# Gate matrix of a PEER layer: one-hots and gates from fp32 to bf16, three exact gate parts, written in pairs of columns

## The chip, the cores and the metric

One core of a Trainium2 chip runs the whole program. The time is device microseconds from launch to the end of one execution. Before the change it is 3040.93 us, the median of 3 runs (3038.23 to 3045.83). The engines are named as in the profile: PE is the matrix engine (PEld its weight loads), DVE the vector engine, ACT the scalar engine, POOL the general-purpose engine, and SP the engine that issues most DMAs.

## The reference, cut to what matters

The program is two transformer blocks in fp32 over 512 tokens of width 1024. Only the last part, the PEER layer of the second block, is touched. For every token, 8 retrieval heads choose 16 experts each out of 16384 = 128 x 128, so a token has 128 slots; slot s names an expert by two indices (i, j) between 0 and 127 and carries a softmax weight, its gate.

```python
gates = jax.nn.softmax(best_s, axis=-1)
...
act = jax.nn.gelu(jnp.einsum('td,thkd->thk', xb, u).astype(jnp.float32))
w = (gb * act).astype(xb.dtype)
return jnp.einsum('thk,thkd->td', w, v)
```

The kernel computes this for 384 of the 512 tokens (three blocks of 128, `NDENSE = 3`) in dense form: it multiplies the tokens with the first matrix of all 16384 experts, applies gelu, multiplies with a gate matrix that is zero where a token has not chosen an expert, and multiplies with the second matrix of all experts. For one token the gate matrix is 128 x 128: entry (i, j) is the sum over the 128 slots of onehot(i)[s] * gate[s] * onehot(j)[s], which is one matmul over the slots. The last 128 tokens fetch their chosen rows by indirect DMA ("gathers") instead.

## The kernel before

The program is written as straight code, and the order on each engine comes from a scheduler that simulates the timeline; blocks marked high priority go first when they are ready, and `issue_after` keeps an instruction behind a named one. The code runs through these stages at the end:

- *Retrieval* (`retrieve`, L1238, and `decode`): scores, the two top-16 searches and the expert indices, on DVE for the most part, with the dense products of experts 0 to 14 beside it on PE.
- *Gate stage*. `slots_T` (L1360) transposes the slots of one token block (i, j, gate) on PE, so that slots lie on partitions and tokens on columns, and ACT copies the result to SBUF as `slT`, in fp32. `gate_matrix` (L1370) then goes through 12 blocks of 32 tokens, each in 8 groups of 4 tokens (96 groups in all, "quads" below). For a quad it needs, per token, a 128 x 128 one-hot matrix of j (`ohB`) and one of i times the gate (`ohA`). Even quads take form A: DVE makes both one-hots in one instruction (L1382, 1024 columns), and ACT multiplies the one of i by the gate, one token at a time (L1384). Odd quads take form D: DVE makes the one-hot of j (L1386, 512 columns) and then, per token, the one of i times the gate in one instruction (L1388). PE multiplies the two, 4 matmuls per quad in fp32 (L1391; the trace has two records for each), into a PSUM tile `pg` of one bank, of which there are 2. ACT copies it to a staging tile (L1393). After 8 quads SP writes the 2 MB staging tile to DRAM (`gd`).
- Beside the gate stage PE makes the dense products of experts 19 to 39 (`expert_act`, L1397: 24 matmuls of 384 columns each, fp32r, L271 to L273, from weights that ACT and POOL split into a high and a low part, L245 and L248). `peer` (L1430) spaces them: gates have high priority, and the product of expert j is kept behind a gate quad that lies 10 quads back (`NLAG`). The last three products come after the last quad.
- *Expert stage*. `open_v` frees the buffers of the gate stage; then for each of 128 groups of experts the gates are read back (`gread`, L1466), multiplied with the activations (L1414), and multiplied with the second matrix. The gathers run beside it. The first `gread` needs all 12 writes to `gd`.

The lines that set the pace of the gate stage:

```python
if GATED[q] == "A":
    nc.vector.tensor_tensor(one, iota(2), sl[:, 0:2, k:k + 4, None]...., op=ALU.is_equal)
    for r in range(4):
        nc.scalar.activation(A4[:, r], one[:, 0, r], AF.Copy, scale=sl[:, 2, ...])
else:
    nc.vector.tensor_tensor(one[:, 1:2], iota(1), sl[:, 1:2, k:k + 4, None]...., op=ALU.is_equal)
    for r in range(4):
        nc.vector.tensor_scalar(A4[:, r], self.iota, ..., op0=ALU.is_equal, op1=ALU.mult)
for r in range(4):
    last = nc.tensor.matmul(p[:, r, :], A4[:, r], one[:, 1, r], start=True, stop=True)
```

Of the kernel before, what the change touches and what calls it, by code (L numbers as in the profile page):

```python
# [11 lines left out]
BF16 = mybir.dt.bfloat16  # L12
U32 = mybir.dt.uint32
AF = mybir.ActivationFunctionType
# [33 lines left out]
GATED = "ADADADAD"  # L48
# [121 lines left out]
class Prog:  # L170
# [1189 lines left out]
    def slots_T(self, i):  # L1360

        nc = self.nc
# [3 lines left out]
        t_ = self.B([128, 3, 128], f"slT{i}", 1)  # L1366
        nc.scalar.activation(t_, p, AF.Copy)
        return t_

    def gate_matrix(self, slT, gd):  # L1370

        nc = self.nc
        for b in range(NDENSE * 4):
            st = self.b("gstage", [128, 128, 32])
            for q in range(8):
                p = self.b("pg", [128, 4, 128])
                t_ = b * 32 + q * 4
                sl, k = slT[t_ // 128], t_ % 128
                A4, one = self.b("ohA", [128, 4, 128]), self.b("ohB", [128, 2, 4, 128])
                iota = lambda n: self.iota[:, None, None, :].to_broadcast([128, n, 4, 128])  # L1380
                if GATED[q] == "A":
                    nc.vector.tensor_tensor(one, iota(2), sl[:, 0:2, k:k + 4, None].to_broadcast([128, 2, 4, 128]), op=ALU.is_equal)  # L1382
                    for r in range(4):
                        nc.scalar.activation(A4[:, r], one[:, 0, r], AF.Copy, scale=sl[:, 2, k + r:k + r + 1])  # L1384
                else:
                    nc.vector.tensor_tensor(one[:, 1:2], iota(1), sl[:, 1:2, k:k + 4, None].to_broadcast([128, 1, 4, 128]), op=ALU.is_equal)  # L1386
                    for r in range(4):
                        nc.vector.tensor_scalar(A4[:, r], self.iota, sl[:, 0, k + r:k + r + 1], sl[:, 2, k + r:k + r + 1],  # L1388
                                                op0=ALU.is_equal, op1=ALU.mult)
                for r in range(4):  # L1390
                    last = nc.tensor.matmul(p[:, r, :], A4[:, r], one[:, 1, r], start=True, stop=True)  # L1391
# [145 lines left out]
def body(tc, I, out, dbg=None, manual=False):  # L1537
    nc = tc.nc
    with ExitStack() as es:
# [121 lines left out]
        P.open(eq1, "retrieve", "xs 7 gb keys q; sc 5; mux 1; ts 2; ti 2; bs 2; bc 2; wk 3; cand 1; tif 1; ab 1; bit 2; cm 1; cu 2; cuf 1; ef 1; gate 1; sel0 1; sel1 1")  # L1661
# [5 lines left out]
        def open_q2():  # L1667
            eq1.close()
            P.open(eg, "gate", "gstage 2; ohA 4; ohB 3")
# [22 lines left out]
```

## Time and profile before

| what | value |
|---|---|
| median of 3 runs | 3040.93 us |
| profiled execution, its own time | 3040.9 us |
| its span (first to last instruction) | 3039.1 us |
| mean granted PE clock | 0.989 of full speed |
| PE / DVE / ACT / POOL busy over the span | 97% / 61% / 41% / 44% |

The profile is of one execution. A busy share is an average over stages that have different limits, so the rows below are cut to the gate stage, which lies between 1935 and 2122 us. "Idle before" is the time in which an engine stood still directly before an instruction, and the arrow names what it waited for. Matmuls overlap, so the time that one occupies PE is the distance between two starts, not its duration; the same holds for DVE instructions that follow each other without a wait.

### The profile page before, as it was taken

The page shows a single profiled execution, that of the slowest core. Times are in us where ns is not written, and L with a number is a line of the kernel's source. Part 1 is how long each engine was busy: PE and PEld are TensorE (multiplying, and loading weights), DVE is VectorE, ACT ScalarE, POOL GpSimd, SP SyncE. Part 2 cuts the span into 40 slices and gives each one's busy share as a digit, 9 for nine tenths or more (in the row PEclk, how much of TensorE's full clock was granted, in tenths as well). Part 3 has the DMA queues.
Part 4 walks back from the last instruction along what each step waited for, and adds up shares of the span by engine and source line. Part 5 has one row for each costly group of instructions (what it writes and reads, how often), then busy time and mean ns, then how long its engine had stood idle before and what let it go on. Part 6 is the DMA issues. An engine that isn't in the chain of part 4 may idle for free.

```text
span 3039.1 us, 40262 instructions
## 1 busy us (share of the span) xinstructions
PE 2938.0 (97%) x15129; PEld 2540.3 (84%) x15129; DVE 1867.7 (61%) x3017; ACT 1245.4 (41%) x2120; POOL 1352.4 (44%) x926
## 2 busy tenths in 40 slices
PE   7998998999999999999999999989999999999998
PEld 6877787888878887888888888888899999999887
DVE  4237664444133663355532489898678877777898
ACT  5455654222232453244432344576333333333333
POOL 3223213222234662233332344422677777777765
PEclk9998999999999999999999999999999999999999
DMA  4220003333332212322233432355988888898987
GB/s 155 63 63 15 1 30 103 97 97 97 97 107 88 63 46 73 108 83 81 82 105 114 130 97 88 125 190 195 303 299 296 311 312 302 289 324 300 320 321 264
DMA packets 174355, 473.60 MB, mean 156 GB/s; under 512 B 15057, under 2 KB 64593, under 8 KB 172625
## 3 DMA queue, kind: packets, MB, share of 16 engines
q1 hardware_dynamic: 137296, 336.80, 34.0%
q0 software_dynamic: 36864, 134.23, 12.5%
q8 instruction: 119, 1.95, 0.3%
q14 instruction: 76, 0.61, 0.1%
HBM read 439.49 MB, written 31.46 MB: 155 GB/s over the span
## 4 chain that ended last, share of the span: by engine, by line
PE 78%; issue 6%; DVE 5%; DMA 5%; ACT 3%; POOL 3%; SPq 0%; POOLq 0%; DVEq 0%; ACTq 0%
PE acc L271 15%; PE acc L272 15%; PE acc L273 15%; DMA urow<-ev,ei 3%; PE A L273 3%; PE A L272 3%; PE A L271 3%; PE B L272 3%; PE B L271 3%; PE B L273 3%; PE pg L1391 2%; PE i L810 2%; POOL urow L1339 1%; DMA rawx<-ev 1%; PE lev L987 1%
## 5 line engine op out<-in xcount | busy, mean ns | idle before, releaser
L248 POOL TENSOR_TENSOR lo<-raw,hi 128x1024 fp32r<-128x1024 f32 x224 | 558.1, 2493 | 946.3 <-ACT hi L245 920.5
L271 PE MATMUL acc<-u,hi 128*128 128x512 f32 (+3 forms) x2344 | 857.6, 367 | 4.0 <-DVE sil L912 1.5
L272 PE MATMUL acc<-u,hi 128*128 128x512 f32 (+3 forms) x2344 | 856.8, 366 | 0.2 <-DVE u L477 0.2
L273 PE MATMUL acc<-u,lo 128*128 128x512 f32 (+3 forms) x2344 | 856.9, 366 | 0.0
L245 ACT ACTIVATE hi<-raw 128x1024 fp32r<-128x1024 f32 x447 | 472.3, 1057 | 901.2 <-PE acc L272 457.4
L248 DVE TENSOR_TENSOR lo<-raw,hi 128x1024 fp32r<-128x1024 f32 x223 | 316.1, 1417 | 297.3 <-ACT hi L245 297.0
L271 PEld LDWEIGHTS acc<-u,hi 128*128 128x128 f32 (+1 forms) x2344 | 443.8, 190 | 59.0 <-issue 2.7
L272 PEld LDWEIGHTS acc<-u,hi 128*128 128x128 f32 (+1 forms) x2344 | 444.1, 189 | 54.7 <-issue 2.7
L273 PEld LDWEIGHTS acc<-u,lo 128*128 128x128 f32 (+1 forms) x2344 | 444.0, 189 | 48.7 <-issue 0.6
L1347 DVE SCALAR_TENSOR_TENSOR urow<-urow,h4row 128x1024 f32<-128x1024 f32 x128 | 200.8, 1575 | 94.5 <-DMA urow<-eu,ei 94.3
L1357 DVE SCALAR_TENSOR_TENSOR po<-urow,act,po 128x1024 f32<-128x1024 f32 x127 | 188.9, 1487 | 66.3 <-DMA urow<-ev,ei 65.4
L1339 POOL DMA_INDIRECT urow<-eu,ei x128 | 188.4, 1472 | 32.9 <-issue 21.4
L1417 ACT ACTIVATE wh<-wf 128x384 fp32r<-128x384 f32 x128 | 67.2, 526 | 312.4 <-PE D L272 246.4
L1339 POOL DMA_INDIRECT urow<-ev,ei x128 | 171.2, 1337 | 43.8 <-DVE po L1357 18.0
L248 POOL TENSOR_TENSOR lox<-rawx,hix 128x1024 fp32r<-128x1024 f32 x53 | 134.8, 2543 | 92.7 <-ACT hix L245 92.5
L1391 PE MATMUL pg<-ohB,ohA 128*128 128x128 f32 x768 | 105.1, 286 | 19.0 <-ACT gstage L1393 17.1
L1391 PEld LDWEIGHTS pg<-ohB,ohA 128*128 128x128 f32 x768 | 98.7, 197 | 24.4 <-ACT gstage L1393 20.9
L1418 DVE TENSOR_TENSOR wl<-wf,wh 128x384 fp32r<-128x384 f32 x128 | 98.8, 773 | 6.8 <-ACT wh L1417 5.1
L1384 ACT ACTIVATE ohA<-ohB,slT 128x128 f32<-128x128 f32 x192 | 61.4, 392 | 41.8 <-DVE ohB L1382 41.7
L1414 DVE TENSOR_TENSOR wf<-eact,gread 128x384 f32<-128x384 f32 x98 | 67.0, 684 | 17.0 <-DMA gread<-gd 15.9
L1388 DVE TENSOR_SCALAR ohA<-iota,slT 128x128 f32<-128x128 f32 x192 | 76.6, 461 | 0.0
L245 ACT ACTIVATE hix<-rawx 128x1024 fp32r<-128x1024 f32 x53 | 55.7, 1052 | 27.4 <-DMA rawx<-ev 27.4
(574 smaller groups left out, 5511.1 us busy)
## 6 DMA issues: line engine op xcount, KB each, us to landing
raw<-ut SPq DMA_DIRECT2D x128, 512.0 KB
raw<-ev SPq DMA_DIRECT2D x75, 512.0 KB
rawx<-ev SPq DMA_DIRECT2D x53, 512.0 KB
raw<-w_ret SPq DMA_DIRECT2D x48, 512.0 KB
gd<-gstage SPq DMA_DIRECT2D x12, 2048.0 KB
gread<-gd SPq DMA_DIRECT2D x32, 768.0 KB
raw<-w_gu SPq DMA_DIRECT2D x44, 512.0 KB
raw<-w_hg SPq DMA_DIRECT2D x32, 512.0 KB
```

Source lines behind the costliest of these rows:

```text
L245: self.nc.scalar.activation(hi, raw, AF.Copy)
L248: r = eng.tensor_tensor(lo, raw, hi.bitcast(F32), op=ALU.subtract)
L271: mm(out, a[0], b[0], start=start, stop=False)
L272: mm(out, a[0], b[1], start=False, stop=False)
L273: return mm(out, a[1], b[0], start=False, stop=stop).ins
L1339: r = nc.gpsimd.indirect_dma_start(out=u, out_offset=None, in_=src, in_offset=bass.IndirectOffsetOnAxis(ap=ei[:, s:s + 1], axis=0))
L1347: nc.vector.scalar_tensor_tensor(u, u, 1.0, row, op0=ALU.mult, op1=ALU.mult, accum_out=act[:, s:s + 1])
L1357: nc.vector.scalar_tensor_tensor(o, u, act[:, s:s + 1], o, op0=ALU.mult, op1=ALU.add)
L1388: nc.vector.tensor_scalar(A4[:, r], self.iota, sl[:, 0, k + r:k + r + 1], sl[:, 2, k + r:k + r + 1], op0=ALU.is_equal, op1=ALU.mult)
L1391: last = nc.tensor.matmul(p[:, r, :], A4[:, r], one[:, 1, r], start=True, stop=True)
L1417: nc.scalar.activation(wh, wf, AF.Copy)
L1418: nc.vector.tensor_tensor(wl, wf, wh.bitcast(F32), op=ALU.subtract)
```

## The change

Two quads (8 tokens) now share their one-hots. `slots_T` leaves the indices as bf16 (`ijT`, exact, being below 256) and splits the gate into three bf16 parts whose sum is the fp32 gate (`gT`): ACT rounds the rest to bf16, DVE subtracts, twice. Once for 128 tokens ACT writes indices and gate parts again with every value twice side by side (`ij`, `g3`), so that the innermost run of every DVE operand is two neighbouring bf16 elements. For 8 tokens DVE then makes both one-hots in one instruction (2048 columns of bf16) and multiplies the one of j by each of the three gate parts (three instructions of 1024 columns). PE runs, per token, three bf16 matmuls with the same one-hot of i as weights, and adds them up in PSUM. The finished quads go to the tile `pg` or `psc` in turn, which makes 4 banks. ACT no longer multiplies by the gate; form A and form D are gone.

```diff
-        t_ = self.B([128, 3, 128], f"slT{i}", 1)
-        nc.scalar.activation(t_, p, AF.Copy)
-        return t_
+        ij, g3 = self.B([128, 2, 128], f"ijT{i}", 1, BF16), self.B([128, 3, 128], f"gT{i}", 1, BF16)
+        nc.scalar.activation(ij, p[:, 0:2], AF.Copy)
+        r = self.b("grest", [128, 128])
+        nc.scalar.activation(r, p[:, 2], AF.Copy)
+        for w in range(3):
+            nc.scalar.activation(g3[:, w], r, AF.Copy)
+            if w < 2:
+                r_ = r
+                r = self.b("grest", [128, 128])
+                nc.vector.tensor_tensor(r, r_, g3[:, w], op=ALU.subtract)
+        return ij, g3
...
+        io = self.b("iotab", [128, 128], BF16)
+        nc.vector.tensor_copy(io, self.iota)
+        pairs = lambda a: a.rearrange("p n (c e) -> p n c e", e=2)
...
+            if b % 4 == 0:
+                ij, g3 = self.b("ij", [128, 16, 2, 8, 2], BF16), self.b("g3", [128, 3, 128, 2], BF16)
+                ij_, g3_ = slT[b // 4]
+                for w in range(2):
+                    nc.scalar.activation(ij[:, :, w], ij_[:, w].rearrange("p (n r) -> p n r", r=8)[:, :, :, None].to_broadcast([128, 16, 8, 2]), AF.Copy)
+                nc.scalar.activation(g3, g3_[:, :, :, None].to_broadcast([128, 3, 128, 2]), AF.Copy)
             for q in range(8):
...
+                k = b % 4 * 32 + q * 4
+                if q % 2 == 0:
+                    one, gb = self.b("ohA", [128, 16, 128], BF16), self.b("ohB", [128, 3, 8, 128], BF16)
+                    nc.vector.tensor_tensor(pairs(one), pairs(io[:, None, :].to_broadcast([128, 16, 128])),
+                                            ij[:, k // 8].rearrange("p w r e -> p (w r) e")[:, :, None, :].to_broadcast([128, 16, 64, 2]),
+                                            op=ALU.is_equal)
+                    for w in range(3):
+                        nc.vector.tensor_tensor(pairs(gb[:, w]), pairs(one[:, 8:16]),
+                                                g3[:, w, k:k + 8, None, :].to_broadcast([128, 8, 64, 2]), op=ALU.mult)
+                p = self.b("pg" if q % 2 else "psc", [128, 4, 128])
                 for r in range(4):
-                    last = nc.tensor.matmul(p[:, r, :], A4[:, r], one[:, 1, r], start=True, stop=True)
+                    for w in range(3):
+                        last = nc.tensor.matmul(p[:, r, :], one[:, q % 2 * 4 + r], gb[:, w, q % 2 * 4 + r],
+                                                start=w == 0, stop=w == 2)
...
-            P.open(eg, "gate", "gstage 2; ohA 4; ohB 3")
+            P.open(eg, "gate", "gstage 2; iotab 1; ij 1; g3 1; ohA 2; ohB 2")
```

The rest of a split, `grest`, lies in a buffer of the retrieval pool, whose memory the gate pool takes over.

## Rows read from the trace of the kernel before

**Rows 1.** Page, busy us and share of the span and instructions of each engine.
```profile
PE 2938.0 (97%) x15129; PEld 2540.3 (84%) x15129; DVE 1867.7 (61%) x3017; ACT 1245.4 (41%) x2120; POOL 1352.4 (44%) x926
```
**Rows 2.** Windows: length, busy PE, PEld, DVE, ACT, POOL (instructions), PE clock, DMA, GB/s.
```profile
1970.00:1990.00 20.00, 17.38 (x127) 16.84 (x126) 19.02 (x34) 14.07 (x35) 4.80 (x3) 1.00 0.60 224
2090.00:2110.00 20.00, 16.32 (x112) 15.58 (x110) 18.12 (x31) 13.74 (x35) 5.30 (x2) 0.92 0.45 158
2200.00:2300.00 100.00, 100.00 (x508) 91.12 (x507) 76.72 (x95) 35.38 (x49) 74.62 (x42) 1.00 0.86 303
```
**Rows 3.** Groups by line, 1935 to 2122 us: busy, mean ns | idle before.
```profile
L1391 PE MATMUL pg<-ohB,ohA 128*128 128x128 f32 x768 | 105.1, 286 | 19.0 <-ACT gstage L1393 17.1 <-ACT ohA L1384 1.3
L1388 DVE TENSOR_SCALAR ohA<-iota,slT 128x128 f32<-128x128 f32 x192 | 76.6, 461 | 0.0
L1382 DVE TENSOR_TENSOR ohB<-iota,slT 128x1024 f32<-128x1024 f32 x48 | 60.0, 1251 | 8.1 <-PE pg L1391 6.5 <-ACT slT L1367 1.1
L1393 ACT ACTIVATE gstage<-pg 128x512 f32<-128x512 f32 x96 | 53.6, 585 | 8.6 <-PE pg L1391 8.2
L272 PE MATMUL acc<-u,hi 128*128 128x384 f32 x130 | 45.0, 346 | 0.0
L1386 DVE TENSOR_TENSOR ohB<-iota,slT 128x512 f32<-128x512 f32 x48 | 43.8, 912 | 6.1 <-ACT ohA L1384 3.6 <-PE pg L1391 1.2 <-issue 1.2
L248 POOL TENSOR_TENSOR lo<-raw,hi 128x1024 fp32r<-128x1024 f32 x17 | 43.2, 2541 | 129.7 <-ACT hi L245 129.7
```
**Rows 4.** Timeline of DVE, two quads without a wait: start, us, engine, line, operation.
```profile
1979.21 1.21 DVE L1382 TENSOR_TENSOR ohB<-iota,slT 128x1024 f32<-128x1024 f32 x1
1980.35 1.10 DVE L1388 TENSOR_SCALAR ohA<-iota,slT 128x128 f32<-128x128 f32 x4
1981.37 0.68 DVE L1386 TENSOR_TENSOR ohB<-iota,slT 128x512 f32<-128x512 f32 x1
1981.97 1.21 DVE L1382 TENSOR_TENSOR ohB<-iota,slT 128x1024 f32<-128x1024 f32 x1
```
**Rows 5.** Timeline, the same DVE line beside a POOL instruction.
```profile
1976.18 2.42 POOL L248 TENSOR_TENSOR lo<-raw,hi 128x1024 fp32r<-128x1024 f32 x1 [6.14 <-ACT hi L245]
...
1975.43 3.26 DVE L1388 TENSOR_SCALAR ohA<-iota,slT 128x128 f32<-128x128 f32 x4
```
**Rows 6.** Timeline of DVE, first and last work of the gate stage, next work behind.
```profile
1935.14 2.75 DVE L1382 TENSOR_TENSOR ohB<-iota,slT 128x1024 f32<-128x1024 f32 x1 [1.15 <-ACT slT L1367]
2117.51 1.12 DVE L1388 TENSOR_SCALAR ohA<-iota,slT 128x128 f32<-128x128 f32 x4
2134.51 1.03 DVE L1414 TENSOR_TENSOR wf<-eact,gread 128x384 f32<-128x384 f32 x2 [15.88 <-DMA gread<-gd]
```
**Rows 7.** Timeline of PE, products of an expert, a run of gate matmuls.
```profile
2094.77 0.34 PE L271 MATMUL acc<-u,hi 128*128 128x384 f32 x1
2094.94 0.34 PE L272 MATMUL acc<-u,hi 128*128 128x384 f32 x1
...
2099.17 1.95 PE L1391 MATMUL pg<-ohB,ohA 128*128 128x128 f32 x16
```
**Rows 8.** Timeline of DVE in the retrieval, three instructions of 128 columns.
```profile
1916.97 0.27 DVE L1288 TENSOR_TENSOR gate<-bs 128x128 f32<-128x128 f32 x1
1917.16 0.22 DVE L1297 TENSOR_SCALAR cm<-bc 128x128 uint32<-128x128 uint32 x1
1917.30 0.23 DVE L1298 TENSOR_SCALAR cu<-bc 128x128 uint32<-128x128 uint32 x1
```
**Rows 9.** Groups by line and shape, whole span, weight loads: busy, mean ns | idle.
```profile
L620 PEld LDWEIGHTS <-identb 128*128 128x128 bf16 x32 | 3.2, 99 | 2.6 <-issue 1.7
L1365 PEld LDWEIGHTS pslT<-ident,sel 128*128 128x128 f32 x6 | 0.8, 154 | 5.4 <-ACT sel L1323 3.5 <-ACT slT L1367 1.7
```
**Rows 10.** Timeline of ACT, first copy of transposed slots, first products with the gate.
```profile
1934.63 0.47 ACT L1367 ACTIVATE slT<-pslT 128x384 f32<-128x384 f32 x1
1941.12 1.27 ACT L1384 ACTIVATE ohA<-ohB,slT 128x128 f32<-128x128 f32 x4
```

More of the change, by code (lines that the diff above doesn't have):

```diff
@@ L47 @@
 IN_ORDER = ((0, 0), (0, 1), (0, 2), (0, 3), (1, 0), (1, 1), (1, 2), (1, 3))
-GATED = "ADADADAD"
 NBESIDE = 15
@@ L1370, in gate_matrix @@
+        return ij, g3
     def gate_matrix(self, slT, gd):
         nc = self.nc
+        io = self.b("iotab", [128, 128], BF16)
+        nc.vector.tensor_copy(io, self.iota)
+        pairs = lambda a: a.rearrange("p n (c e) -> p n c e", e=2)
         for b in range(NDENSE * 4):
             st = self.b("gstage", [128, 128, 32])
-            for q in range(8):
[L1376 to L1389, printed above, removed]
@@ L1660, in body @@
         eq1 = ExitStack()
-        P.open(eq1, "retrieve", "xs 7 gb keys q; sc 5; mux 1; ts 2; ti 2; bs 2; bc 2; wk 3; cand 1; tif 1; ab 1; bit 2; cm 1; cu 2; cuf 1; ef 1; gate 1; sel0 1; sel1 1")
+        P.open(eq1, "retrieve", "xs 7 gb keys q; sc 5; mux 1; ts 2; ti 2; bs 2; bc 2; wk 3 grest; cand 1; tif 1; ab 1; bit 2; cm 1; cu 2; cuf 1; ef 1; gate 1; sel0 1; sel1 1")
         P.banks("A psc; C pslT; B pg")
```

## The prediction

> **What bounds the kernel now.** I read the page's busy shares first: PE is at 97% over the span [rows 1], so a change that frees PE looks welcome. The windows cut that down. In the expert stage, 2200 to 2300, PE is busy for all of 100 us; in the gate stage PE is at 17.38 of 20 us, and the engine near its limit is DVE, 19.02 of 20, with ACT at 14.07 [rows 2]. So the stage that the change touches is set by another engine than the page names.
>
> The groups of that stage confirm it. DVE has 48 instructions of 1024 columns, 48 of 512 and 192 of 128, busy for 60.0, 43.8 and 76.6 us, and stands still for only 8.1 + 6.1 = 14.2 us [rows 3]. From its first gate instruction to the end of its last, 1935.14 to 2118.63, are 183.5 us [rows 6].
>
> I split these 183.5 us by distances between starts. Two quads in a row cost 1.14 us (1979.21 to 1980.35), 1.02 and 0.60, together 2.76 [rows 4]; 48 times that is 132.5. Idle is 14.2. What is left, 36.8 us, is something that only some instructions pay. One group of four, 1.10 us long when alone [rows 4], takes 3.26 where a POOL split of 2.42 us runs beside it [rows 5], which is 2.16 more. There are 17 such splits in the stage [rows 3], and 17 x 2.16 = 36.7. So DVE is made of work 132.5, blocking by POOL 36.8 and idle 14.2, and the first two are no one's slack.
>
> What the end of this stage costs the program is one for one. The next DVE work, at 2134.51, waits for a read of the gates [rows 6], which needs the last quad written to DRAM, and behind it PE has no gap into which a delay could go [rows 2]. I add any shift of the stage's end to the whole time.
>
> **The change part by part.** *DVE, two quads.* One compare of 2048 bf16 columns, three products of 1024. No row shows a two-operand bf16 instruction, so I bound it. From 0.60 us for 512 fp32 columns and 1.14 for 1024 [rows 4] a column costs 1.055 ns. If a bf16 column costs the same, the four take 1.14 + 1024 x 0.001055 = 2.22, and 3 x 1.14, together 5.64 us for two quads. If bytes decide, they are the instructions of 1024 and 512 fp32 columns: 1.14 + 3 x 0.60 = 2.94. The trace has a hint that DVE can do two results in a step: the one-operand instruction of 128 columns follows the one before after 0.14 us, the two-operand one of 128 columns needs 0.19 [rows 8], where the fp32 slope for 64 columns is 0.07. I take 2.94, since the operands are laid out in pairs of neighbours that fill one 4-byte word, and keep 5.64 as a rival. A third value below 2.94 would need four results in a step; no row excludes it, and it enters the faster rival. So 48 x 2.94 = 141.1 us, which is 8.6 more than the 132.5 of now. The count of instructions falls from six to four for two quads, but the columns make up for it.
>
> The Trainium skill, "VectorE: DVE Perf Modes", section "Mode 2×_1P — pack two bf16 into one 32-bit read", says that a two-operand instruction gets two results in a cycle if all operands are 16-bit with step one, and one result otherwise. No run so far shows it; by it the pairs would give the 2.94, and a layout without pairs the 5.64.
>
> *Blocking by POOL.* The 17 splits stay. All DVE instructions of a pair now have two operands in SBUF; the two-operand form is blocked like the other now (the means of L1382 and L1386, 1251 and 912 ns, lie above their 1.21 and 0.68 alone [rows 3, 4]). I leave 36.8 us. Below, the blocking could shrink if a packed read leaves room; above, it could hit no more than 17 times 2.42.
>
> *Extra DVE work.* Six subtractions for the three parts and one copy of the table, 7 x 0.19 [rows 8] = 1.4 us.
>
> *PE.* Now 768 records. A run of 16 takes 1.95 us, less the duration of the last, 0.28, over 15 distances: 0.11 us each [rows 7, 3], 85 us in all. The products beside them come every 0.17 us [rows 7], some 387 of them (three groups of about 130 [rows 3]), 66 us. After it there are 96 x 12 = 1152 bf16 matmuls of 128 columns. By columns alone 0.17 / 3 = 0.057 us each; at most the 0.11 of the fp32 records, since each still loads its own weights. An isolated bf16 load is 99 ns and an fp32 one 154 [rows 9]; 0.11 scaled by that is 0.07, which I take: 81 us, and with 66 beside it 147 us in 183. PE is then nearer to 80% than 90% of the stage, and that gain goes nowhere as long as DVE is later: its cover is DVE's 2.94 + 36.8 / 48 = 3.71 us for two quads against PE's 24 x 0.07 + 66 / 48 = 3.06.
>
> The Trainium skill, "TensorE: Matmul & The Clock Gate", section "LDWEIGHTS (loading the stationary operand)", prices a load by its columns, 128 / 1.2 GHz = 107 ns, whatever the contraction; by that 1152 loads would be 123 us where its section on fast weight load would halve them. Rows 9 show a shorter bf16 load, but none back to back.
>
> *ACT and banks.* ACT loses 192 products of the gate and gets five small copies and three widening ones for each 128 tokens; it has 6 of 20 us free now [rows 2], so nothing is counted. With it go the waits of DVE on ACT's `ohA`, 3.6 us, and on PE's `pg`, 6.5 + 1.2 [rows 3]; the second bank takes the 17.1 us that PE waits for the copies out of PSUM [rows 3]. But the new buffers hold two pairs, and DVE must wait for PE's 24 matmuls of the pair before the last, in an order that mixes them with the products of 0.17. And the widened indices and gates have one buffer, so twice, at each new 128 tokens, DVE waits for ACT's refill. I take 5 us of idle, between 0 and the 14.2 of now.
>
> *Start.* Now ACT's first copy of transposed slots begins at 1934.63 and DVE starts 0.5 us later; the first products with the gate on ACT come at 1941.12 [rows 10, 6]. After it a chain of rounding and subtracting between ACT and DVE, three rounds long, stands ahead of the first product with a gate part, and the rest of a split lies in memory that the new one-hot buffers may take over, which then wait for the third block's chain. At ACT's 0.5 us and DVE's 0.27 [rows 10, 8] a round is under 1 us. I take 2 us, between 0 and 5.
>
> *Sum.* 141.1 + 36.8 + 1.4 + 5 + 2 = 186.3 us against 183.5: 2.8 later. The profiled execution took 3040.9 us, of which 1.8 lie outside its span of 3039.1, the median of the runs being 3040.93. So 3040.9 + 2.8 = 3044 us. With idle and start at their ends (0 and 0, 14.2 and 5) the stage is 179.3 to 198.5 us, the time 3037 to 3056.
>
> **The rivals.** *Columns, not bytes.* If DVE doesn't pack, the stage is 48 x 5.64 = 270.7, + 36.8 + 1.4 + 2, nothing idle: 311 us, 127 more, 3168 us. For it speaks that no packed two-operand instruction is in the trace; against it the layout in pairs and rows 8. Slower.
>
> *Weight loads bind PE.* At 0.11 us a matmul PE needs 127 + 66 = 193 us, and starts some 6 us after DVE: 199, or 15 more, 3056 us. It decides from 0.10 us a matmul on, where PE's two quads cost DVE's 3.71. For it speaks that every matmul loads weights anew, three times the same; against it the shorter load of rows 9.
>
> *DVE falls below PE.* If the packed instructions cost less than their bytes, or POOL blocks them for less, DVE's 178 us shrink until PE's 147 bind, with 6 us of start and a tail of quads without products beside them (the window at 2090 to 2110 is of that kind, clock 0.92 [rows 2]): some 160 us, 23 less, 3018 us. For it speaks that nothing in the trace shows these forms; against it that fp32 instructions of both kinds paid the full price of a POOL split.
>
> **How the numbers follow.** The measurement of this kernel can tell about 0.3%, 9.1 us, from no change: faster is below 3031.8, slower above 3050. The forecast (DVE stays the bound, 3037 to 3056) has 0.50, the unpacked rival 0.12, the weight loads 0.16, the faster one 0.22. Of the forecast 0.41 lies within the bound, 0.02 below and 0.07 above; of the weight loads 0.04 within; of the faster one 0.02. So faster 0.22, same 0.47, slower 0.31. The range goes from 3015, a little under the faster rival's value, to 3064, which holds the weight loads with a few us of start; left out are the unpacked case and a little at the ends. The likeliest one's own range is 3037 to 3056.
>
> **What would show it.** Starts of DVE's new instructions 1.14 and 0.60 us apart: bytes decide; 2.2 and 1.14: columns. DVE still some 2.2 us longer beside each POOL split. Distances of bf16 matmuls near 0.07 us, and PE idle in the stage grown to 30 us or more with DVE as what it waits for. First to last gate instruction of DVE about 186 us, and behind it the same distances to the first read of the gates as now. I am wrong if DVE has more than 20 us of idle in the stage, if the gate matmuls come 0.1 us apart, or if the expert stage changes its length by more than the shift.

## The result: 0.7% slower, and the profile after

The changed kernel takes 3062.56 us (median of 4 runs, 3061.87 to 3067.23), the kernel before beside it 3043.38 (4 runs, 3038.23 to 3046.05). The ratio is 1.0068, 95% interval 1.005 to 1.0087. The forecast was 3044: no change that can be told, where the kernel became slower. The time lies inside the range of 3015 to 3064, and above the likeliest case's own range of 3037 to 3056.

The profiled execution took 3067.23 us, with a span of 3065.4, which is 26.3 more than before. It is the longest of the four; between the medians lie 19.2 us. The page's busy shares (answer to [rows 1]) hardly tell the two apart:

```profile
PE 2934.2 (96%) x15513; PEld 2525.9 (82%) x15513; DVE 1879.1 (61%) x2928; ACT 1197.3 (39%) x1949; POOL 1358.1 (44%) x926
```

The windows do (answer to [rows 2], columns as there; the third is later by about the shift):

```profile
1970.00:1990.00 20.00, 15.04 (x149) 13.74 (x148) 17.38 (x18) 7.06 (x12) 4.82 (x2) 0.93 0.47 167
2090.00:2110.00 20.00, 18.85 (x170) 16.72 (x170) 17.46 (x22) 7.59 (x14) 3.27 (x2) 0.84 0.33 132
2225.00:2325.00 100.00, 100.00 (x507) 91.04 (x506) 75.44 (x94) 35.27 (x48) 74.14 (x42) 1.00 0.87 302
```

DVE fell from 19.02 and 18.12 busy us to 17.38 and 17.46, and PE's granted clock from 1.00 and 0.92 to 0.93 and 0.84. Over the eight windows of 20 us from 1950 to 2110 the clock's mean is 0.885, where it was 0.99. It has two levels, 1.2 and 2.4 GHz; 0.885 is a mixture in time. The expert stage is as full as before. The groups of the gate stage, 1935 to 2146 (answer to [rows 3], columns as there), name who waits for whom:

```profile
L1402 DVE TENSOR_TENSOR ohB<-ohA,g 128x1024 bf16<-128x1024 bf16 x144 | 110.4, 822 | 1.6
...
L1398 DVE TENSOR_TENSOR ohA<-iotab,ij 128x2048 bf16<-128x2048 bf16 x48 | 70.2, 1464 | 18.1 <-PE pg L1407 14.8 <-PE psc L1407 2.1 <-ACT ij L1392 0.8
L1407 PE MATMUL psc<-ohB,ohA 128*128 128x128 bf16 x576 | 59.5, 238 | 30.0 <-DVE ohB L1402 30.0
L1407 PE MATMUL pg<-ohB,ohA 128*128 128x128 bf16 x576 | 58.0, 235 | 15.3 <-DVE ohB L1402 15.3
...
L247 POOL TENSOR_TENSOR lo<-raw,hi 128x1024 fp32r<-128x1024 f32 x17 | 42.3, 2485 | 150.6 <-ACT hi L244 150.6
```

L1398 is the compare (`ohA`, both one-hots), L1402 a product with a gate part (`ohB`), L1407 the gate matmuls. PE waits 45 us for DVE, which it may, being the faster of the two. But DVE, the slower, waits 18.1 us too, nearly all of it for PE to release `ohA`. Each waits for the other.

DVE's last pairs and the first work behind the stage (answer to [rows 4] and [rows 6]; start, us, engine, line):

```profile
2132.34 1.22 DVE L1398 TENSOR_TENSOR ohA<-iotab,ij 128x2048 bf16<-128x2048 bf16 x1
2133.59 1.90 DVE L1402 TENSOR_TENSOR ohB<-ohA,g 128x1024 bf16<-128x1024 bf16 x3
2135.41 1.22 DVE L1398 TENSOR_TENSOR ohA<-iotab,ij 128x2048 bf16<-128x2048 bf16 x1
...
2139.72 1.90 DVE L1402 TENSOR_TENSOR ohB<-ohA,g 128x1024 bf16<-128x1024 bf16 x3
2158.24 1.03 DVE L1431 TENSOR_TENSOR wf<-eact,gread 128x384 f32<-128x384 f32 x2 [16.61 <-issue]
```

A pair without a wait is 2135.41 - 2132.34 = 3.07 us. The stage goes from 1944.90 (the first compare, below) to 2139.72 + 1.90 = 2141.62, that is 196.7 us against 183.5. So the 26.3 us are: 9.8 of later start (1944.90 against 1935.14 [rows 6]), 13.2 of longer stage, 0.7 from its end to the first read gate (16.6 against 15.9), and 2.6 in the rest of the program.

The start, on DVE:

```profile
1933.96 0.23 DVE L1331 CAST ei<-ef 128x128 uint32<-128x128 f32 x1
1935.75 1.41 DVE L1375 TENSOR_TENSOR grest<-grest,gT 128x128 f32<-128x128 f32 x1 [1.56 <-ACT gT L1371]
1937.54 0.29 DVE L1375 TENSOR_TENSOR grest<-grest,gT 128x128 f32<-128x128 f32 x1 [0.38 <-ACT gT L1371]
1940.69 1.38 DVE L1375 TENSOR_TENSOR grest<-grest,gT 128x128 f32<-128x128 f32 x1 [2.87 <-ACT gT L1371]
...
1943.62 0.29 DVE L1375 TENSOR_TENSOR grest<-grest,gT 128x128 f32<-128x128 f32 x1 [0.38 <-ACT gT L1371]
1943.83 0.22 DVE L1383 CAST iotab<-iota 128x128 bf16<-128x128 f32 x1
1944.90 2.36 DVE L1398 TENSOR_TENSOR ohA<-iotab,ij 128x2048 bf16<-128x2048 bf16 x2 [0.85 <-ACT ij L1392]
```

All six subtractions, those of the second and third block too, stand in front of the first compare, most of them waiting for ACT. From the end of retrieval (the cast `ei`) to the first gate instruction it is 10.94 us; before it was 1.37.

What the clock does inside the stage can be read on PE. These rows are a gate matmul behind a wait, ten gate matmuls at full clock, twenty at half, then expert products:

```profile
1984.85 0.22 PE L1407 MATMUL psc<-ohB,ohA 128*128 128x128 bf16 x1 [2.46 <-DVE ohB L1402]
...
1986.01 0.72 PE L1407 MATMUL pg<-ohB,ohA 128*128 128x128 bf16 x10
...
1989.65 1.22 PE L1407 MATMUL pg<-ohB,ohA 128*128 128x128 bf16 x10 [0.23 <-DVE ohB L1402]
1990.67 1.27 PE L1407 MATMUL psc<-ohB,ohA 128*128 128x128 bf16 x10
1991.70 0.67 PE L270 MATMUL acc<-u,hi 128*128 128x384 f32 x1
1992.17 0.52 PE L271 MATMUL acc<-u,hi 128*128 128x384 f32 x1
1992.49 0.52 PE L272 MATMUL acc<-u,lo 128*128 128x384 f32 x1
...
1994.68 0.34 PE L272 MATMUL acc<-u,lo 128*128 128x384 f32 x1
1994.86 0.34 PE L270 MATMUL acc<-u,hi 128*128 128x384 f32 x1
```

The granted clock of three stretches among them is 1.00, 0.50 and 1.00 (third number from the end):

```profile
1986.00:1986.80 0.80, 0.73 (x14) 0.56 (x10) 0.77 (x2) 0.59 (x2) 0.00 (x0) 1.00 0.94 271
1989.70:1994.00 4.30, 4.30 (x28) 3.99 (x28) 3.69 (x6) 1.20 (x2) 0.00 (x0) 0.50 0.01 4
1994.70:2000.00 5.30, 5.30 (x61) 4.81 (x60) 3.79 (x6) 1.90 (x4) 0.00 (x0) 1.00 0.46 195
```

Ten in 0.72 us, less the last one's 0.22, over nine distances are 0.055 us each; ten in 1.27, less 0.31, are 0.107. Products come 0.32 apart (1992.17 to 1992.49) instead of 0.18 (1994.68 to 1994.86). From the wait ahead of the first row up to 1989.65 PE had stood still for 2.46, 0.33, 0.59, 1.34 and 0.23 us, waiting for `ohB`; the longest wait is the one in which a POOL split of 2.44 us held up DVE's products (first row below, 4.04 us for 1.90). DVE pays two pairs later:

```profile
1981.36 4.04 DVE L1402 TENSOR_TENSOR ohB<-ohA,g 128x1024 bf16<-128x1024 bf16 x3
...
1993.24 1.90 DVE L1402 TENSOR_TENSOR ohB<-ohA,g 128x1024 bf16<-128x1024 bf16 x3
1996.54 1.23 DVE L1398 TENSOR_TENSOR ohA<-iotab,ij 128x2048 bf16<-128x2048 bf16 x1 [1.41 <-PE pg L1407]
```

This holds for the whole stage. Of the 17.0 us for which DVE waits for PE, 15.2 lie in a stretch at half clock or within 3 us behind the end of one; such stretches, with these 3 us, are 76 of the stage's 197 us.

The account of the stage is then 48 x 3.07 = 147.4 us of work; blocking by POOL, read from the means of the groups over an undisturbed 1.22 and 0.685, 48 x 0.244 + 144 x 0.137 = 31.4; and what is left of 196.7, 17.9, is idle (the trace has 18.8 between the first compare and the last product).

### The profile page after: what moved, and what is told of

It reads as the page before. It is cut to its first block, busy times and chain, and to the rows that moved or that the text cites. A ratio compares the mean times of both kernels' runs of the same rounds, so it can differ in the third digit from the quotient of the medians.

```text
span 3065.4 us, 40567 instructions
## 1 busy us (share of the span) xinstructions
PE 2934.2 (96%) x15513; PEld 2525.9 (82%) x15513; DVE 1879.1 (61%) x2928; ACT 1197.3 (39%) x1949; POOL 1358.1 (44%) x926
## 5 line engine op out<-in xcount | busy, mean ns | idle before, releaser
L1356 DVE SCALAR_TENSOR_TENSOR po<-urow,act,po 128x1024 f32<-128x1024 f32 x127 | 206.1, 1623 | 69.3 <-DMA urow<-ev,ei 68.5
L1338 POOL DMA_INDIRECT urow<-ev,ei x128 | 179.4, 1401 | 40.0 <-issue 20.6
L247 POOL TENSOR_TENSOR lox<-rawx,hix 128x1024 fp32r<-128x1024 f32 x53 | 135.9, 2564 | 87.3 <-ACT hix L244 87.0
L1407 PEld LDWEIGHTS <-ohA 128*128 128x128 bf16 x1152 | 76.1, 107 | 60.4 <-issue 41.9
L1402 DVE TENSOR_TENSOR ohB<-ohA,g 128x1024 bf16<-128x1024 bf16 x144 | 110.4, 822 | 1.6
L1435 DVE TENSOR_TENSOR wl<-wf,wh 128x384 fp32r<-128x384 f32 x128 | 85.5, 670 | 5.7 <-ACT wh L1434 5.7
L1407 PE MATMUL psc<-ohB,ohA 128*128 128x128 bf16 x576 | 59.5, 238 | 30.0 <-DVE ohB L1402 30.0
L1431 DVE TENSOR_TENSOR wf<-eact,gread 128x384 f32<-128x384 f32 x98 | 75.4, 770 | 17.7 <-issue 16.6
L1398 DVE TENSOR_TENSOR ohA<-iotab,ij 128x2048 bf16<-128x2048 bf16 x48 | 70.2, 1464 | 18.1 <-PE pg L1407 14.8
L1407 PE MATMUL pg<-ohB,ohA 128*128 128x128 bf16 x576 | 58.0, 235 | 15.3 <-DVE ohB L1402 15.3
```

What stands on the lines that cost most here:

```text
L247: r = eng.tensor_tensor(lo, raw, hi.bitcast(F32), op=ALU.subtract)
L1338: r = nc.gpsimd.indirect_dma_start(out=u, out_offset=None, in_=src, in_offset=bass.IndirectOffsetOnAxis(ap=ei[:, s:s + 1], axis=0))
L1356: nc.vector.scalar_tensor_tensor(o, u, act[:, s:s + 1], o, op0=ALU.mult, op1=ALU.add)
L1402: nc.vector.tensor_tensor(pairs(gb[:, w]), pairs(one[:, 8:16]), g3[:, w, k:k + 8, None, :].to_broadcast([128, 8, 64, 2]), op=ALU.mult)
L1407: last = nc.tensor.matmul(p[:, r, :], one[:, q % 2 * 4 + r], gb[:, w, q % 2 * 4 + r], start=w == 0, stop=w == 2)
L1431: nc.vector.tensor_tensor(wf.rearrange("p (b t) -> p b t", t=32), a.rearrange("p (b t) -> p b t", t=32), gr[:, :, j % 4, :], op=ALU.mult)
```

## The experiments

Two theories about the two terms that had failed, and their rivals. *Clock*: with bf16 gates PE has so little to do that it stands still between them, the granted clock falls to half, and at half clock PE releases the one-hots late, so DVE waits. Rivals: too few banks, or simply the order of PE's work. *Start*: the rest of the split lies in memory that `ohA` takes over, so the first compare waits for the third block's split. Rival: the chain to the first block takes that long anyway. Where an expectation uses letters, A and B in e_psum are the theory of the start and its rival, C and D in e_extra the theory of the clock and the rival of PE's order; the A of e_split0 is the blocking by POOL. All times are medians, with the ratio to the kernel before in the same series. The stage is that of the profiled execution, from the start of the first compare to the end of the last product; the kernel before has 183.5 us.

| kernel | us | ratio | interval | stage, us |
|---|---|---|---|---|
| changed kernel | 3062.6 | 1.0068 | 1.0050 to 1.0087 | 196.7 |
| e_extra: one more matmul per token | 3048.4 | 1.0019 | 1.0006 to 1.0032 | 180.9 |
| e_two: one matmul fewer | 3061.6 | 1.0064 | 1.0047 to 1.0082 | 192.9 |
| e_aord: order held by hand | 3063.1 | 1.0074 | 1.0060 to 1.0088 | 197.1 |
| e_aordx: the same order, one more matmul | 3053.1 | 1.0043 | 1.0030 to 1.0057 | 187.9 |
| e_xord: the order of e_extra, nothing added | 3074.9 | 1.0111 | 1.0096 to 1.0127 | 211.0 |
| e_onebank: the doubled banks undone | 3070.0 | 1.0078 | 1.0051 to 1.0104 | 201.8 |
| e_psum: rest of the split in PSUM | 3062.3 | 1.0062 | 1.0039 to 1.0085 | 197.6 |
| e_xpsum: e_extra and e_psum | 3042.4 | 1.0004 | 0.9994 to 1.0014 | 181.0 |
| e_cols: no pairs | 3170.1 | 1.0431 | 1.0415 to 1.0447 | 303.9 |
| e_raw: e_xpsum, compare in two halves | 3044.6 | 1.0019 | 1.0009 to 1.0030 | 180.4 |
| e_split0: weight splits on DVE | 3034.3 | 0.9978 | 0.9965 to 0.9991 | 176.2 |
| e_best: e_split0 and e_extra | 3034.2 | 0.9981 | 0.9970 to 0.9993 | 173.7 |
| e_psplit0: e_split0 and e_psum | 3030.9 | 0.9966 | 0.9952 to 0.9979 | 177.7 |
| e_bestp: all three | 3030.9 | 0.9976 | 0.9965 to 0.9988 | 173.9 |
| e_bsplit0: kernel before, splits on DVE | 3031.6 | 0.9971 | 0.9960 to 0.9982 | 175.4 |

**More work for PE.** The edit repeats the first matmul of each token; its result is overwritten.

```diff
-                    for w in range(3):
-                        last = nc.tensor.matmul(..., start=w == 0, stop=w == 2)
+                    for n, w in enumerate((0, 0, 1, 2)):
+                        last = nc.tensor.matmul(..., start=n < 2, stop=n in (0, 3))
```

> The changed kernel with one more bf16 matmul per token: the first gate part is multiplied twice, and the second pass overwrites the first, so PE has 4 matmuls per token and DVE, ACT and POOL have the same work. DVE stands still for 18.1 us in the changed kernel, 17 of them behind PE's release of the one-hots, and the granted clock in the stage is 0.83 to 0.93 in most windows. Theory C (PE has too little work, its clock falls while it waits for DVE, and it then gives the buffers back late): the clock of the windows rises towards 1.0, DVE's idle time falls by 5 us or more, and the time stays or falls by up to 8 us. Theory D (PE is late because its matmuls stand in a fixed order behind products of an expert, with its own work on the path): 384 more matmuls of 0.055 us, 21 us of PE work, raise DVE's idle time by 3 to 12 us and the time by as much.

384 matmuls whose result is overwritten make the kernel 14 us faster (3062.6 to 3048.4), more than the 8 us at most that theory C gave. The windows and groups of this kernel:

```profile
1970.00:1990.00 20.00, 18.79 (x214) 17.52 (x214) 19.83 (x22) 8.74 (x15) 5.99 (x2) 1.00 0.42 159
...
L1402 DVE TENSOR_TENSOR ohB<-ohA,g 128x1024 bf16<-128x1024 bf16 x144 | 121.9, 901 | 1.7
L1398 DVE TENSOR_TENSOR ohA<-iotab,ij 128x2048 bf16<-128x2048 bf16 x48 | 58.4, 1218 | 3.4 <-PE pg L1407 2.5 <-ACT ij L1392 0.8
```

The clock is 1.00 in each of the seven windows from 1950 to 2090 and 0.99 in the next, DVE is busy for 19.83 of 20 us, and its idle falls from 18.1 to 3.4. The blocking by POOL is still whole: 144 x (0.901 - 0.685) = 31.1 us. With 147.4 of work, 180.9 - 147.4 - 31.1 leaves 2.4 us idle in the stage (the trace has 4.2).

**Less work for PE.** The loop runs over the first two gate parts only.

> The changed kernel, but PE multiplies only the first two gate parts (the third part is left out of the result; DVE still makes it). PE has 384 bf16 matmuls fewer in the gate stage, everything else is the same. Theory of the clock: what DVE waits for is a PE that is slow because it is lightly loaded, so taking work from it doesn't help: granted clock 0.9 or lower in most windows of the stage, DVE idle before the compare 15 us or more, time 3058 to 3070 us, against 3062 of the changed kernel. Rival, the amount of PE work: 384 x 0.055 to 0.107 is 21 to 41 us of PE time gone, DVE's idle falls under 10 us and the time to 3045 to 3055 us.

The kernel is not faster by more than the intervals tell (1.0064 against 1.0068), with 384 matmuls gone:

```profile
1970.00:1990.00 20.00, 13.14 (x114) 11.40 (x113) 19.96 (x22) 8.19 (x14) 6.26 (x2) 0.85 0.50 177
2090.00:2110.00 20.00, 16.13 (x124) 15.38 (x122) 15.98 (x20) 6.41 (x12) 2.51 (x1) 0.74 0.33 132
...
L1398 DVE TENSOR_TENSOR ohA<-iotab,ij 128x2048 bf16<-128x2048 bf16 x48 | 59.5, 1264 | 17.4 <-PE pg L1407 16.4 <-ACT ij L1392 0.9
```

The clock is lower still, and DVE waits as long for a PE with a third less to do in the gates. The amount of PE work, as the rival had it, is ruled out. All 16.4 us of waiting for PE lie in a stretch at half clock or within 3 us behind one.

**Order or clock.** In e_extra the scheduler, which prices the added matmuls, had also put the expert products elsewhere: some 22 behind each 64 gate matmuls and six pairs without products at the end, where the changed kernel has runs of up to 72 and eight pairs at the end. Three kernels hold the order by hand, each matmul queued behind the one before it in the list (the edit in short):

```diff
+        for i, n in enumerate(runs):        # lengths of the runs of gate matmuls and products in turn
+            for _ in range(n):
+                if i % 2 == 0:
+                    with self.tc.high_priority():
+                        next(gm)            # one gate matmul, issue_after(the last product)
+                else:
+                    self.behind = next(ea)  # one product, issue_after(the last gate matmul)
```

> A control. The changed kernel with its own order of gate matmuls and expert products on PE written out by hand and held by ordering edges, no added work. Both theories (clock, order): as the changed kernel, 3058 to 3068 us, DVE idle before the compare 15 us or more. If the time differs, the holding itself costs something, and the two runs beside it are to be compared with this one.

3063.1 us: holding the order costs nothing.

> The same order held by hand, that of the changed kernel, with one more matmul per token in front of its three. Theory of the clock: the added work alone keeps the clock at 1.00, DVE idle falls under 6 us, time 3045 to 3053 us. Rival, the order: the kernel with one more matmul also had the expert products spread more evenly between the gates (22 products behind each 64 matmuls, 6 pairs of groups without products at the end, against runs of 72 and 8 pairs at the end), and that was what helped; then this run stays at 3058 to 3068 us, or above.

3053.1 us, 10 less than its control, at the upper edge of what the clock theory gave. Its condition on DVE's idle failed: 15.1 us where under 6 was expected, against 21.1 in the control. The clock in the eight windows is 1.00 in four and 0.91 to 0.98 in the others:

```profile
L1398 DVE TENSOR_TENSOR ohA<-iotab,ij 128x2048 bf16<-128x2048 bf16 x48 | 71.2, 1489 | 15.1 <-PE pg L1413 14.3 <-ACT ij L1392 0.8
```

The idle that is left is for the most part not the clock's. In the control 18.2 of the 19.6 us of waiting for PE lie at half clock or within 3 us behind it; here it is 1.9 of 14.3. The others are waits for a PE at full clock, which in this order has up to 96 gate matmuls in a row. Nor are the 9.2 us between the two stages the clock's alone: the idle inside the stage fell by 5.5, and by the distances between starts the blocking by POOL by 3.7.

> The order of gates and expert products of the kernel with one more matmul, held by hand, but with the changed kernel's three matmuls per token. Theory of the clock: PE has as little to do as in the changed kernel, the granted clock stays at 0.9 or so, DVE idle 12 us or more, time 3056 to 3066 us. Rival, the order: the even spread alone gives 3045 to 3053 us.

3074.9 us, the slowest of the five. The even order alone is worse by 12 us than the old one, not better, and 9 us above what the clock theory gave for it:

```profile
1970.00:1990.00 20.00, 14.71 (x155) 13.49 (x155) 16.28 (x16) 7.00 (x13) 4.91 (x2) 0.90 0.42 157
...
L1398 DVE TENSOR_TENSOR ohA<-iotab,ij 128x2048 bf16<-128x2048 bf16 x48 | 57.9, 1221 | 33.7 <-PE pg L1410 32.7 <-ACT ij L1392 0.9
```

Of 32.8 us of waiting for PE 31.9 lie at half clock or within 3 us behind it. So the order as rival is out as the cause of the gain. In either order the added work raises the clock and takes time away, 10 us in the old order and 26 in the even one (3074.9 to e_extra's 3048.4, of another series). How much a fallen clock costs does depend on the order; why the even one pays more is not shown.

**Banks.** All finished quads go to `pg`, so that there are two banks again.

```diff
-                p = self.b("pg" if q % 2 else "psc", [128, 4, 128])
+                p = self.b("pg", [128, 4, 128])
```

> The changed kernel with the doubling of banks undone: all quads go to the tile pg, 2 banks as in the kernel before. If the second tile is worth what the change meant (PE waited 17.1 us for ACT's copies before it), the time rises by 5 to 12 us, to about 3070, and PE waits for gstage again. If PE has so much slack that the banks don't matter, the time stays within 4 us of 3062 and no wait of PE for gstage over 5 us shows.

3070.0 us; the intervals overlap with the changed kernel's. In the profile the stage is 5 us longer and PE waits 8.1 us for the copies out of PSUM. Doubling the banks is no cause of the loss; it is worth some us, which these runs don't settle.

**Start.** The rest of the split goes to a free PSUM bank.

```diff
-        r = self.b("grest", [128, 128])
+        R = self.b("grest", [128, 3, 128])      # in PSUM
+        r = R[:, 0]
...
-                r = self.b("grest", [128, 128])
+                r = R[:, w + 1]
```

> The changed kernel, with the rest of the gate split (grest) kept in an unused PSUM bank in place of the retrieval pool's memory. The changed kernel's first compare starts at 1944.90, 9.8 us later than the first one-hot of the kernel before (1935.14), right behind the last subtraction of the third block. Theory A (the memory that the gate pool takes over is held by the third block's split): the first compare now starts at about 1938, 6 to 8 us earlier, and the time falls by as much, to about 3055 us. Rival B (the late start is the chain of rounding itself, or ACT's order): the first compare stays within 2 us of 1944.9 and the time within 3 us of 3062. The idle time of DVE behind PE later in the stage stays at 15 to 20 us by both.

In the trace the first compare now comes in front of the third block's subtractions:

```profile
1930.24 0.23 DVE L1331 CAST ei<-ef 128x128 uint32<-128x128 f32 x1
...
1937.28 2.36 DVE L1399 TENSOR_TENSOR ohA<-iotab,ij 128x2048 bf16<-128x2048 bf16 x2
1939.56 0.29 DVE L1376 TENSOR_TENSOR grest<-grest,gT 128x128 f32<-128x128 f32 x1
```

It is 7.04 us behind the cast where it was 10.94, so the edit takes 3.9 of the 9.6 us away. That is not the memory alone, since subtractions in PSUM aren't held up beside a POOL split either (0.30 us where two took 1.41 and 1.38), while the cast of the table now is (1.14 us for 0.22). Two runs below keep the splits off POOL and part the two: the distance is 8.79 us with the memory as it was (e_split0) and 6.07 without (e_psplit0). By them 2.2 us of the 9.6 go with the splits on POOL and 2.7 with the memory; 4.7, which no edit here takes away, are the chain itself. The time did not move (3062.3; in the traces the stage is 0.9 us longer), so neither A nor B holds whole: the compare came earlier, and the gain did not reach the end. Beside the added matmul some of it may:

> The changed kernel with one more matmul per token (clock at full speed) and with the rest of the gate split held in PSUM, so that the first compare does not wait for the third block's split. Theory of the start: the first compare comes some 4 us earlier after the index copy, the stage keeps its 181 us, and the time is 3.9 us under that of the extra matmul alone: 3042 to 3046 us against 3048. Rival: the earlier start is given back inside the stage, and the time is 3047 to 3050 us.

3042.4 us, ratio 1.0004 (0.9994 to 1.0014), against 1.0019 (1.0006 to 1.0032) for the added matmul alone. The two intervals overlap, so the gain (6 us by medians, 3.9 by the start) is likely rather than shown. What is shown is that both edits together bring the kernel back to the time of before.

**Pairs.** Same buffers, but the innermost step of index and gate part is 0 over 128 columns (the edit in short).

```diff
-  tensor_tensor(pairs(one), pairs(io...), ij[...][:, :, None, :].to_broadcast([128, 16, 64, 2]), is_equal)
+  tensor_tensor(one, io..., ij[...][:, :, 0:1].to_broadcast([128, 16, 128]), is_equal)
```

(and the products in the same way)

> The changed kernel with the operands not taken in pairs: the compare and the products read the same bf16 buffers, but index and gate part stand still for 128 columns (innermost step 0) in place of pairs of neighbours. Theory (the pairs are what lets DVE make two results in a step): the compare takes some 2.2 us in place of 1.21 and a product some 1.14 in place of 0.68, the stage is 270 us of DVE work and more, the time 3145 to 3170 us. Rival (16-bit operands pack in any layout): compare and product as in the changed kernel, 3062 us.

3170.1 us. DVE's rows:

```profile
2211.81 2.36 DVE L1402 TENSOR_TENSOR ohB<-ohA,g 128x1024 bf16<-128x1024 bf16 x2
2214.09 2.28 DVE L1398 TENSOR_TENSOR ohA<-iotab,ij 128x2048 bf16<-128x2048 bf16 x1
```

A product takes 1.14 us (2.28 from start to start for two) instead of 0.60, a compare 2.28 instead of 1.22. The prediction's unpacked rival gave 3168 for this case, from the fp32 slope of [rows 4].

**The late first product.** On top of e_xpsum the compare is split in two, the one-hots of j first (the edit in short).

```diff
-  one compare of [128, 16, 128]
+  for w in (1, 0):
+      compare of one[:, w * 8:w * 8 + 8]
```

> The changed kernel with one more matmul per token and the rest of the split in PSUM (3042 us), and the compare in two halves, the one-hots of j first and those of i behind, so that the first product reads what the instruction before the last wrote. Theory (the 0.12 us that the first product comes late is the wait for the result of the instruction directly before): the distances are 0.60, 0.60 and 3 x 0.60, a pair 3.0 us in place of 3.07, and the time 3038 to 3042 us. Rival (the 0.12 us belongs to the change from compare to product, or to another halt): a pair is 3.1 us or more, the time 3042 to 3047 us.

```profile
2089.33 1.28 DVE L1400 TENSOR_TENSOR ohA<-iotab,ij 128x1024 bf16<-128x1024 bf16 x2
2090.53 1.89 DVE L1404 TENSOR_TENSOR ohB<-ohA,g 128x1024 bf16<-128x1024 bf16 x3
2092.34 1.28 DVE L1400 TENSOR_TENSOR ohA<-iotab,ij 128x1024 bf16<-128x1024 bf16 x2
```

The pair is 3.01 us: 1.20 for two halves, then 1.81, with no 0.12 between compare and product. So that 0.12 was the wait for the result of the instruction directly in front, as the theory said. The time did not follow, 3044.6 us where the theory gave 3038 to 3042: DVE's idle rose from 1.7 to 12.6 us, 12.5 of it for `pg`. With four matmuls per token PE is the next bound.

**POOL's splits moved to DVE.** Beside the gate stage the weight splits run on DVE.

```diff
+        self.pool_split = 0
         for j in range(NEARLY, NFIFO):
```

> The changed kernel with the weight splits of the gate stage's products on DVE (1.14 us each by the distance of its starts) in place of POOL. Theory A (each POOL split blocks DVE for 2.2 us, 15 to 17 of them, 33 to 37 us in the stage): DVE gives up 33 us of blocking for 17 x 1.14 = 19 us of work, and PE no longer starves for 2 us at a time; the stage is 14 to 25 us shorter, the time 3037 to 3048. Rival: POOL's blocking was hidden behind waits for PE, and the work on DVE adds up: the time rises by 5 to 19 us, to 3067 to 3081.

3034.3 us, 28 less than the changed kernel, under the kernel before and 3 us under what the theory gave. Its groups:

```profile
L1402 DVE TENSOR_TENSOR ohB<-ohA,g 128x1024 bf16<-128x1024 bf16 x144 | 90.4, 688 | 1.1
...
L1398 DVE TENSOR_TENSOR ohA<-iotab,ij 128x2048 bf16<-128x2048 bf16 x48 | 57.8, 1223 | 13.1 <-PE pg L1407 10.1 <-ACT gstage L1410 1.9 <-ACT ij L1392 0.8
```

Means of 688 and 1223 ns: no blocking is left. The clock is still 0.90 in the mean of the eight windows, and DVE idle 13.1 us.

> The changed kernel with both edits that helped: the weight splits beside the gate stage on DVE itself in place of POOL, and one more matmul per token. Theory: the two losses are separate, blocking of DVE by POOL and waiting of DVE for a slowly clocked PE, so the gains add: the stage falls from 176 us (splits on DVE) by the some 10 us of DVE idle to about 166 us, clock 1.00, time 3020 to 3028 us. Rival: with the blocking gone PE never starves for 2 us and the clock costs nothing any more, or the added PE work becomes the bound: time 3032 to 3038 us, as with the splits on DVE alone.

3034.2 us: the rival was right, the gains don't add. The clock is 1.00 in all eight windows, but the stage is only 2.5 us shorter than in e_split0, with 9.4 us of idle in front of the compare, and PE busy for 19.47 of 20 us in three of the windows. The added work has become PE's bound.

> The changed kernel with the weight splits beside the gate stage on DVE in place of POOL, and the rest of the gate split in PSUM. Theory: with the splits on DVE (3034 us) the earlier start is worth the 4 to 6 us that it was worth beside the extra matmul: 3027 to 3031 us. Rival: with the clock at times at half speed, as it still is with the splits on DVE, the earlier start is lost again inside the stage, as it was in the changed kernel: 3033 to 3036 us.

> The changed kernel with all three: splits on DVE, rest of the gate split in PSUM, one more matmul per token. Theory: splits on DVE with the extra matmul (3034 us) have PE at 97% busy in the stage, so PE has become the bound, and an earlier start of the gate matmuls moves the end by the start alone: 3028 to 3032 us. Rival: PE's order of expert products sets the end, whatever the start: 3033 to 3036 us.

Both 3030.9 us (3027 to 3037 and 3029 to 3041). They agree with an earlier start by some 3 us; their intervals overlap with e_split0's and e_best's.

> The kernel before, with the weight splits beside the gate stage on DVE in place of POOL, nothing else. Theory: blocking by POOL cost the kernel before the 36.8 us that the prediction gave it; with 17 to 22 splits of 1.2 us on DVE in its place, 20 to 28 us, the stage is 9 to 16 us shorter: 3024 to 3031 us. Then the edit, not the bf16 gate matrix, is what beats the kernel before. Rival: the kernel before loses as much by the added DVE work as it gains: 3036 to 3043 us.

3031.6 us, just above what the theory gave. The stage is 8.1 us shorter than before, not 9 to 16:

```profile
L1382 DVE TENSOR_TENSOR ohB<-iota,slT 128x1024 f32<-128x1024 f32 x48 | 58.6, 1221 | 13.6 <-PE pg L1391 13.6
L1388 DVE TENSOR_SCALAR ohA<-iota,slT 128x128 f32<-128x128 f32 x192 | 53.4, 341 | 0.0
L1386 DVE TENSOR_TENSOR ohB<-iota,slT 128x512 f32<-128x512 f32 x48 | 33.0, 687 | 8.9 <-PE pg L1391 8.1
L248 DVE TENSOR_TENSOR lo<-raw,hi 128x1024 fp32r<-128x1024 f32 x19 | 24.5, 1291 | 12.4 <-ACT hi L245 12.4
```

By the distances between starts the gate instructions occupy 135.9 us of the stage, where it was 170.5: 34.6 us of blocking go. Of the 19 splits in the row 15 lie inside the stage and take 17.0 us. Idle inside the stage rises from 13.0 to 22.4 us, nearly all of it waits for PE's release of the one-hots. That is 34.6 - 17.0 - 9.4 = 8.2 us, against 8.1 between the two ends. The fp32 kernel with this one line is as fast as the best bf16 version: the gain is that of the line, not of the gate matrix.

## Why the prediction was wrong, step by step

- *What bounds the stage, and one for one*: right, to within 3.3 us. The last product came 23.0 us later, the first read of the gates 23.7, the end of the span 26.3.
- *Bytes decide*: right. Starts of products are 0.60 us apart, and e_cols gives the price of the other case. The Trainium skill, "VectorE: DVE Perf Modes", section "Mode 2×_1P — pack two bf16 into one 32-bit read", asks for 16-bit operands with step one; by that rule e_cols had to fall to one result in a step, and the run agrees, with 1.14 us against 0.60. Missed were 0.12 us between compare and first product: 3.07 a pair, not 2.94, 5.8 us in all.
- *Blocking by POOL*, 36.8: 31.4 measured. A compare beside a split takes 3.41 us, still some 2.2 more. Mis-sized was the count: 15 splits lie in the stage, not 17, at some 2.1 us each. Two more run before the first compare, where they hold up two subtractions.
- *PE at 0.07 us a matmul*: 0.055 at full clock, 0.107 at half. The rival in which weight loads bind PE was to decide from 0.10 on. It doesn't hold at full clock; e_two, with a third fewer of these loads, is no faster. The Trainium skill, "TensorE: Matmul & The Clock Gate", section "Wait — 56ns, not 53.3ns?", gives 55.6 and 106.7 ns from start to start at the two clocks; the trace agrees with both. The 107 ns a load that the prediction quoted from the Trainium skill are not seen at full clock; the half of it, quoted there too, is not contradicted.
- *"That gain goes nowhere as long as DVE is later"*: this is the step that failed. I compared DVE's 3.71 us for two quads with PE's 3.06 as though PE kept its clock. With the measured distances PE needs 24 x 0.055 + 7.5 x 0.17 = 2.6 us a pair at full clock (360 products lie between 48 pairs), so by this estimate it stands still for some 30% of DVE's 3.71; in the groups above it waits 45.3 us for DVE. The longest wait in the rows above comes while a split blocks DVE. Then the clock falls, and a pair costs 24 x 0.107 + 7.5 x 0.32 = 5.0 us, more than DVE's. The slack that was to cover PE is what takes its cover away. So the *idle term*, 5 us between 0 and 14.2, is 17.9 us by the account of the stage, and 2.4 where the clock was held up (e_extra). The 14.2 of before takes in 1.15 us ahead of the first instruction [rows 6]; inside the stage it was 13.0.
- *Start*, 2 us between 0 and 5: 9.6. The duration of a round was right (ACT's and DVE's 0.31 and 0.29 us); mis-sized was how many stand in front. I counted one block's chain. By the order on DVE all three blocks' stand there, two subtractions are themselves blocked by a split (1.41 and 1.38 us), and ACT has a weight split and a copy of an expert between the first two blocks. The memory, which I had named, is 2.7 us of it (e_split0 to e_psplit0), the splits on POOL 2.2.
- *Sum*: 186.3 us were forecast for stage and start. With 9.6 of start for 2, 17.9 of idle for 5, 5.8 for the late product, 5.4 less of blocking and the 1.4 of subtractions inside the start it is 186.3 + 7.6 + 12.9 + 5.8 - 5.4 - 1.4 = 205.8; measured are 196.7 + 9.6 = 206.3. With the idle gone and the start cut to 5.6 us (e_xpsum) stage and start are 181.0 + 7.0 - 1.4 = 186.6 us, and the time is that of before. That this is the forecast's 186.3 is in part luck: 5.8 for the late product and 3.6 more of start stand against less blocking and less idle than the sum had.
- *The rivals*: none named this mechanism. Two changed the price of DVE's work and one raised that of PE's; that a PE with less to do could slow the stage stands in none of them. That the time lies inside the range of 3015 to 3064 is luck, since its upper end was set for the weight loads. The conditions for being wrong came near (18.1 + 1.6 us of DVE idle where 20 were named; matmuls 0.107 apart, for part of the stage).

## What to carry to other kernels

Where two engines hand buffers to each other, the faster one's slack is not free if that engine is PE: price its work at the half clock as well, and if that comes out above the other engine's, its idle can come back as the other's wait. Look first at what makes the slower engine irregular; here one line that moves the splits from POOL to DVE was worth more than the rewritten stage. And where a chain between two engines is put in front of a loop, count it for all the blocks that the queue holds, not for the first.

## What the hardware showed that I had not expected

- In this stage 384 matmuls with no use lower the time by 14 us (interval of the ratios 1.0050 to 1.0087 and 1.0006 to 1.0032), the granted clock in the stage going from 0.885 to 1.00.
- DVE instructions in 16 bits, with half the bytes read per column, pay the whole of a POOL split like the fp32 ones: 3.41 us for 1.22.
- An instruction on DVE that reads what the one directly before it wrote starts 0.12 us later; one instruction between them hides it (3.07 to 3.01 us a pair, the second compare costing 0.06).
- bf16 matmuls of 128 columns with a new weight load each come every 0.055 us at full clock, where a third of a product of 384 columns, by columns alone, is 0.057: the loads cost nothing that can be seen.
